# Moving the decay work of two of five token pieces out of the projection stage and into the first eight recurrence steps

## The chip, the cores and the metric

The kernel is one launch on one core of a Trainium2 chip. The metric is the device time of that launch in microseconds (us). The kernel before took 1749.78 us as the median of three runs (1746.99 to 1754.63).

The engines are named as in the profile: PE (TensorE, matmul), PEld (its weight loads), DVE (VectorE), ACT (ScalarE), POOL (GpSimd) and SP (SyncE, which here issues nearly all DMAs from one queue, in order).

## The reference, cut to what matters

One layer of a diffusion backbone over 1024 latent tokens and 256 context tokens of width 1024. One input projection is split between a short convolution group and a bidirectional RWKV-7 group of 8 heads of 64; both are concatenated, projected and added to the input, and a gated MLP with a 3x3 depthwise convolution follows. What matters here is the RWKV part:

```
cb, cc, cx, r, k, v, w_lo, a_lo, g_lo = split(h @ w_in)
kk = k * k_k, normalized over each head
for d in 0, 1:                       # forward and backward in time
    decay = exp(-c * sigmoid(w0[d] + tanh(w_lo) @ w_up[d]))
    a     = sigmoid(a0[d] + a_lo @ a_up[d])
    k_d   = k * (1 + (a - 1) * k_a)
    # per token, state S of each head (64 x 64):
    S = S * decay - (S kk) (kk a)^T + v k_d^T ;   y = S r
```

The context is scanned first, in both directions; the latent scans start from its final states. The backward scan runs from the last latent token to the first.

## The kernel before, in words

Every matmul of weights is done in three products of high and low parts of both operands. The program is written with a library that gives each tile its buffers and orders each engine's instructions by a planner of its own; each engine then runs its instructions strictly in that order and waits on semaphores. The order that is on the chip is therefore fixed when the program is built.

The stages, in order:

1. Modulation vectors and the normalized input (`norm_x`), until about 76 us of the profile.
2. Projections `proj` (L339 to L351), 24 matmuls for each block of 128 columns and 512 tokens. `k_cols` (L392) and `v_cols` (L440) come first, mixed with the rest of the modulation (`ada_rest`) and the normalization of k (`unit_k`), in the order of the string `OR1` (L46). v is transposed to token-major on PE and stored.
3. Decays. The 1280 tokens fall into five pieces of 256, named by their first tile of 128 tokens: piece 0 is the context, pieces 2, 4, 6 and 8 are the latents. `decays` (L520) does, for one piece, eight groups: four pairs of heads `j`, two directions `d` each. A group is four matmuls into `plo` (L551, L552), two tanh on ACT (L555), a sum and a scan on DVE (L558, L560 or L562), two exponentials on ACT (L566, L567), scaled copies of kk, r, k and b on POOL and DVE (L571 to L579), sixteen small matmuls into two `px` tiles (L597), their masking on DVE into `xa` and `xrO` (L599, L601), four transposes into `pt` (L605) and a copy (L607). The results go to memory (`ar_dram`, `xr_dram`, `kb_dram`).
4. Inversion. `invert` (L648) inverts the 64 x 64 triangular systems of one piece that `decays` left in `xa`. On DVE: a transpose, 30 pairs of multiply and add (L666, L668), each of which needs the one before, and two transposes. Then two rounds of small matmuls on PE, `pq` (L684) and `pr` (L691), with copies by ACT between them, and a store to `xa_dram` (L696).
5. The other projections: r and the gate (`r_and_gate`, L796) and the convolution group (`conv_group`, L809), 17 blocks of columns. In the program they stand between and after the pieces 0, 2, 8, 4, 6; the planner fills them in beside the decays.
6. Recurrence. `steps` (L712) does one step: one chunk of 64 tokens forward and one backward. It loads the chunk's data (`cxa` from `xa_dram`, `ckb`, `car`, `cxr`, `vu`), then `ry` (L733, L741), a copy `rh` (L743), `pu` (L750), a copy `vu` (L755, L757), `ps` (L764) and the state update `S` (L767), each waiting for the one before; `ry` (L773) gives y. Steps 1 to 4 are the context (piece 0), steps 5 to 8 need pieces 2 (forward) and 8 (backward), and from step 9 on one direction needs piece 4 and the other piece 6. There are 20 steps. `fill` (L701) puts parts of other work, held in the list `pend`, behind a step's matmuls, in the numbers given by `sl`: first the output product of the convolution group (`conv_out`, L882, tiles `pco`), later the rest of the output (`mix`, `outp`, `to_h2`).
7. The MLP (`pf`, L1038 and L1118), and the final norm.

PSUM has eight banks, and a `Banks` object (L112) says which banks serve which tile name. In the decay stage `B1` (L42) gives `px` banks 4, 5 and 1, `pl` (the tiles `plo` and `pbn`) banks 6 and 7, and `pq` bank 0. Two names on one bank take it in the order in which the program asks for it.

The lines on which the order of the stages rests:

```
decay_and_invert(0)                      # L839
...
for ti in (2, 8, 4, 6):
    decay_and_invert(ti)
...
for r in range(4):                       # L985: the context steps
    steps(ring, [(0, r // 2, r % 2), (1, 1 - r // 2, 1 - r % 2)], ppc, 1)
...
for r in range(16):                      # L992: the latent steps
```

Of the kernel before, what the change touches and what calls it, by code (L numbers as in the profile page):

```python
# [28 lines left out]
TAIL = {10: "m3 m4", 11: "o3 o4 h3 h4", 12: "m2 m5", 13: "o2 o5 h2 h5", 14: "m1 m6", 15: "o1 h1 o6 h6", 16: "m0 m7", 17: "o0 o7", 18: "h0 h7"}  # L29
SL = ((3, 2, 0, 1),) * 10 + ((4, 4, 4, 4),) * 6  # L30
RC = 9
EI = 3
FAST, FQ = (0, 7), (1,)
B5 = dict(pm=(5, 7), px=(0, 4), ph=(4, 0))
YT = 3
IB = 2
XB, XT = 2, 3
# [3 lines left out]
AE = (0, 1, 0, 1, 0, 0, 1, 0)  # L41
B1 = ((4, 5, 1), (2, 3), (6, 7), (0,), (1,))  # L42
B2 = ((2, 3), (1, 6))
B3 = (7, 5)
PA, PL1 = (0,), (6,)
OR1 = "k0 k1 a k2 a k3 a u 0 a u a 1 u a a x 2 a 3"  # L46
B4 = dict(pm=(5, 7), px=(0,), ph=(4,))
# [39 lines left out]
def hybrid_kernel(  # L87
# [238 lines left out]

    cols = [3072] + [b + 128 * j for b in (2048, 2560, 1536) for j in range(4)] + [3200]
    cols += [b + 128 * j for j in range(4) for b in (512, 1024, 0)]
# [30 lines left out]
    def stg():  # L359
        return sg_.tile([128, 512], F32, name="stg", bufs=STG)  # L360
# [38 lines left out]
    def unit_k():  # L399
# [7 lines left out]
        for t0, nt in ((0, 2), (2, 4), (6, 4)):  # L407
# [30 lines left out]
            yield  # L438

    def v_cols(j):  # L440
        for t0, n, p in proj(pp, 2560 + 128 * j, True, 6):
            vt = stg()
            A.copy(vt[:, :n], p[:, :n])
            vm = stg().rearrange("p (t n) -> p t n", n=128)
            nt = n // 128
            pv = pp.tile([128, 512], F32, name="pv", tag="pv", bufs=2)
            for q in range(nt):
                PE.transpose(pv[:, 128 * q:128 * q + 128], vt[:, 128 * q:128 * q + 128], ident)
            V.tensor_copy(vm[:, :nt, :], pv[:, :n].rearrange("p (t n) -> p t n", n=128))
            SY.dma_start(vd[t0 // 128:t0 // 128 + nt, :, 128 * j:128 * j + 128].rearrange("t p n -> p t n"), vm[:, :nt, :])  # L450
# [69 lines left out]
    def decays(pp, pieces):  # L520


        for ti in pieces:
# [4 lines left out]
            for j in range(4):  # L528
# [265 lines left out]

    ppc = Banks(px=B1[0], pj=B1[1], pl=B1[2], pq=B1[3], ry=B1[4], pu=B1[4])
    def r_and_gate():  # L796
        for j in range(4):
            for t0, n, p in proj(ppc, 1536 + 128 * j, False, 6):
                rt = stg()
                A.copy(rt, p)  # L800
                SY.dma_start(rd[j, :, t0 - CTX:t0 - CTX + n], rt)
            yield
# [4 lines left out]
        yield  # L807

# [46 lines left out]
    sh2 = ExitStack()  # L855
    h2p = sh2.enter_context(tc.tile_pool(name="h2p", bufs=1, side="left", reuse_waits="tile"))
    h2 = [[h2p.tile([128, 8, 512], F32R, name=f"h2{hf}{i}") for i in range(2)] for hf in range(2)]
    so = ExitStack()
    ow = so.enter_context(tc.tile_pool(name="ow", bufs=1, side="left", reuse_waits="tile"))

# [324 lines left out]
```

## Time and profile before

| | |
|---|---|
| median of 3 runs | 1749.78 us |
| the profiled execution | 1747.66 us |
| its span, first to last instruction | 1745.9 us |
| PE busy | 1588.5 us (91% of the span) |
| DVE busy | 1146.1 us (66%) |
| ACT busy | 565.3 us (32%) |
| POOL busy | 610.4 us (35%) |
| mean granted PE clock | 0.933 |
| share of the chain that ended last | PE 67%, DVE 18%, DMA 6%, issue 3%, ACT 3%, POOL 2% |

Times are of one execution, read by the hardware profiler. A matmul's busy time overlaps with the next one's, so the pace of PE is read from the starts of its rows. "Granted clock" is 1.0 where PE ran at 2.4 GHz and 0.5 where it ran at 1.2 GHz; a stretch's value is the mean.

### The profile page before, as it was taken

The numbers are of one execution on the slowest core, as the hardware profiler recorded it, in microseconds if no ns is written. First come the engines' busy times: TensorE is split into PE (matmuls) and PEld (weight loads), VectorE is DVE, ScalarE is ACT, GpSimd is POOL, SyncE is SP. The second block draws the span as 40 slices with busy tenths as digits, with TensorE's granted clock in tenths as the row PEclk, the third lists the DMA queues.
The fourth block names the chain that finished last, engine by engine and source line by source line (L and its number), as shares of the span: only waits on it lengthen the run. The fifth ranks groups of instructions, "written<-read, shape, count | busy, mean of one in ns | idle before, by whom it ended". The sixth has DMA issues, their size and how long they took to land.

```text
span 1745.9 us, 27316 instructions
## 1 busy us (share of the span) xinstructions
PE 1588.5 (91%) x10639; PEld 1272.3 (73%) x10639; DVE 1146.1 (66%) x1791; ACT 565.3 (32%) x994; POOL 610.4 (35%) x519
## 2 busy tenths in 40 slices
PE   7699999989898967698687999999999999999997
PEld 2588778777777766577565777888888888788886
DVE  5953525799999983333677667766666666545645
ACT  2644315544535323211133332111111111334423
POOL 2343313333333224723443422222222222545643
PEclk9799799989889966889889999999999999999999
DMA  9294536557667387789863421111111111533531
GB/s 316 99 298 153 178 124 186 180 156 218 203 187 233 103 254 234 244 259 291 266 209 120 128 70 37 49 48 49 49 47 40 47 48 49 169 109 118 172 97 61
DMA packets 237178, 257.41 MB, mean 147 GB/s; under 512 B 18932, under 2 KB 172105, under 8 KB 237049
## 3 DMA queue, kind: packets, MB, share of 16 engines
q1 hardware_dynamic: 236664, 255.51, 46.9%
q8 instruction: 84, 1.38, 0.3%
q14 instruction: 46, 0.37, 0.1%
q0 software_dynamic: 384, 0.15, 0.0%
HBM read 184.04 MB, written 71.57 MB: 146 GB/s over the span
## 4 chain that ended last, share of the span: by engine, by line
PE 67%; DVE 18%; DMA 6%; issue 3%; ACT 3%; POOL 2%; SPq 1%; DVEq 0%; POOLq 0%; ACTq 0%
PE pf L1038 26%; PE pf L1118 14%; PE pj L350 12%; DVE ti L668 3%; DVE tmp L666 3%; PE pco L878 2%; PE po L878 2%; DMA araw<-in_ada_w_dram 2%; PE px L597 1%; DVE acc L1085 1%; PE ry L741 1%; DMA xo<-in_w_out_dram 1%; PE pu L750 1%; PE ps L764 1%; DVE xrO L601 1%
## 5 line engine op out<-in xcount | busy, mean ns | idle before, releaser
L1038 PE MATMUL pf<-h,fhi 128*128 128x512 f32 x1408 | 395.7, 397 | 6.0 <-DVE act L1090 3.4
L1038 PEld LDWEIGHTS pf<-h,fhi 128*128 128x128 f32 x1408 | 264.6, 188 | 70.3 <-DVE act L1090 3.8
L350 PE MATMUL pj<-hx,whi 128*128 128x512 f32 (+1 forms) x976 | 303.4, 390 | 1.5 <-DVE hx L324 1.5
L1085 DVE SCALAR_TENSOR_TENSOR acc<-gp,prm,acc 128x1024 f32<-128x1024 f32 x176 | 270.5, 1538 | 6.0
L105 POOL TENSOR_TENSOR flo<-fraw,fhi 128x1024 fp32r<-128x1024 f32 x50 | 139.1, 2782 | 331.5 <-ACT fhi L104 323.1
L1038 PE MATMUL pf<-h,flo 128*128 128x512 f32 x704 | 227.5, 395 | 0.5 <-POOL flo L105 0.5
L350 PEld LDWEIGHTS pj<-hx,whi 128*128 128x128 f32 x976 | 185.4, 198 | 38.3 <-issue 4.2
L350 PE MATMUL pj<-hx,wlo 128*128 128x512 f32 (+1 forms) x488 | 189.7, 389 | 0.0
L1118 PE MATMUL pf<-dhi,ahl 128*128 128x512 f32 x640 | 163.2, 389 | 0.0
L1038 PEld LDWEIGHTS pf<-h,flo 128*128 128x128 f32 x704 | 132.5, 188 | 34.0 <-POOL flo L105 0.8
L1110 DVE TENSOR_TENSOR ahl<-act,ahl 128x512 fp32r<-128x512 f32 x44 | 86.3, 1971 | 97.2 <-ACT ahl L1109 97.2
L104 ACT CAST fhi<-fraw 128x1024 fp32r<-128x1024 f32 x50 | 52.5, 1049 | 285.8 <-issue 164.4
L1118 PEld LDWEIGHTS pf<-dhi,ahl 128*128 128x128 f32 x640 | 120.1, 188 | 25.4 <-DVE ahl L1110 0.4
L105 POOL TENSOR_TENSOR dlo<-fraw,dhi 128x1024 fp32r<-128x1024 f32 x40 | 98.1, 2458 | 88.5 <-ACT dhi L104 88.4
L105 POOL TENSOR_TENSOR wlo<-wraw,whi 128x1024 fp32r<-128x1024 f32 x26 | 63.9, 2458 | 168.5 <-ACT whi L104 168.4
L1083 DVE TENSOR_SCALAR acc<-gp,prm 128x1024 f32<-128x1024 f32 x22 | 42.6, 1936 | 111.6 <-ACT gp L1075 111.6
L350 PEld LDWEIGHTS pj<-hx,wlo 128*128 128x128 f32 x488 | 96.4, 198 | 17.5 <-issue 1.7
L1118 PE MATMUL pf<-dlo,ahl 128*128 128x512 f32 x320 | 89.1, 389 | 0.0
L597 PE MATMUL px<-arO,kbO 64*128 64x128 f32 (+1 forms) x640 | 66.5, 318 | 18.9 <-DVE xrO L601 12.1
L597 PEld LDWEIGHTS px<-arO,kbO 64*128 64x128 f32 x640 | 54.0, 214 | 35.5 <-issue 29.2
L104 ACT CAST dhi<-fraw 128x1024 fp32r<-128x1024 f32 x40 | 41.9, 1047 | 107.0 <-PE pf L1118 87.5
L760 POOL TENSOR_TENSOR S<-S,pcs 128x512 f32<-128x512 f32 x38 | 41.2, 1099 | 95.8 <-PE ry L741 94.9
(280 smaller groups left out, 2649.2 us busy)
## 6 DMA issues: line engine op xcount, KB each, us to landing
araw<-in_ada_w_dram SPq DMA_DIRECT2D x48, 512.0 KB, 5.2
fraw<-in_ffn_w_up_dram SPq DMA_DIRECT2D x46, 512.0 KB, 3.9
fraw<-in_ffn_w_down_dram SPq DMA_DIRECT2D x44, 512.0 KB, 3.6
wraw<-in_w_in_dram SPq DMA_DIRECT2D x26, 512.0 KB, 4.5
lu<-lu_dram SPq DMA_DIRECT2D x20, 512.0 KB, 5.2
kb_dram<-kbT SPq DMA_DIRECT2D x40, 256.0 KB, 2.7
xa_dram<-xa SPq DMA_DIRECT2D x20, 512.0 KB, 4.8
cxa<-xa_dram SPq DMA_DIRECT2D x40, 256.0 KB, 4.2
```

The source lines that it names most:

```text
L104: A.copy(hi, src)
L105: G.tensor_tensor(out=lo, in0=src, in1=hi.bitcast(F32), op=ALU.subtract)
L350: PE.matmul(p[:, :n], w[:, k, :], hsl(i, k, t0, n), start=(k == 0 and first), stop=(k == 7 and last))
L597: PE.matmul(px[:, ch, i, 0:w], kbO[r, i, 2 * ch:2 * ch + 2, :].rearrange("p s n -> p (s n)"), rhs, start=True, stop=True)
L666: V.tensor_tensor(out=tv, in0=ti[:, j + 1:32, j:j + 1].to_broadcast([128, m, j]), in1=ti[:, j:j + 1, 0:j].to_broadcast([128, m, j]), op=AL ...
L668: V.tensor_tensor(out=ti[:, j + 1:32, 0:j], in0=ti[:, j + 1:32, 0:j], in1=tv, op=ALU.add)
L878: m = PE.matmul(po, hl[:, a_, k, :], w[k][b_][:, sl], start=(k == 0 and f), stop=(k == 3 and l))
L1038: PE.matmul(pts[hf], w[:, k, :], h2[hf][i_][:, k, :], start=(k == 0 and f), stop=(k == 7 and l))
L1083: V.tensor_scalar(out=acc, in0=src, scalar1=wcol, scalar2=prm[:, P_FB + f:P_FB + f + 1], op0=ALU.mult, op1=ALU.add)
L1085: V.scalar_tensor_tensor(out=acc, in0=src, scalar=wcol, in1=acc, op0=ALU.mult, op1=ALU.add)
L1110: V.tensor_tensor(out=hl[:, 1, :], in0=asl, in1=hl[:, 0, :].bitcast(F32), op=ALU.subtract)
L1118: PE.matmul(pd[i], hl[:, a_, 128 * q:128 * q + 128], w[w_][:, 512 * nh:512 * nh + 512], start=(f == 0 and s_), stop=(f == NF - 1 and l_))
```

## The change

The pieces are prepared in another order and at another place.

- The r projections move to stage 2, where the v projections were (`OR1`, `r_cols`, `cols`); the v projections move behind the decays of the end pieces.
- Of the decays and inversions, pieces 0, 2 and 8 alone stand in the program ahead of the recurrence, and behind them v, the gate and the convolution group.
- Pieces 4 and 6 become a generator, `rest`. After each of the first eight steps five parts of it are issued (`PCS`); a piece has 8 parts of decays and 11 of inversion. Steps 9 to 20 come when `rest` is empty, and the second half of the output weights (`wr`) is loaded between.
- In the first eight steps a fill of 1, 1, 0, 1 (`SL0`) parts of `conv_out` stands behind each step's matmuls, from the first step on.
- Banks: in the decay stage `pl` has bank 6 alone and `pv` bank 7; in the first eight steps `px` has banks 4 and 5, and bank 7 serves `pl` and `pq` both.
- Buffers: the inversion's tiles go from two buffers to one (`IB`), `dr` to one, and `rk` shares the buffer of `db`.

```
-IB = 2
+SL0, PCS = (1, 1, 0, 1), 5
+IB = 1
-B1 = ((4, 5, 1), (2, 3), (6, 7), (0,), (1,))
+B1 = ((4, 5, 1), (2, 3), (6,), (0,), (7,))
-OR1 = "k0 k1 a k2 a k3 a u 0 a u a 1 u a a x 2 a 3"
+OR1 = "k0 k1 a k2 a k3 a u r0 a u a a r1 u a a x r2 r3"
-    cols = [3072] + [b + 128 * j for b in (2048, 2560, 1536) for j in range(4)] + [3200]
+    cols = [3072] + [b + 128 * j for b in (2048, 1536, 2560) for j in range(4)] + [3200]
+    def r_cols(j):
+        for t0, n, p in proj(pp, 1536 + 128 * j, False, 6):
+            rt = stg()
+            A.copy(rt, p)
+            SY.dma_start(rd[j, :, t0 - CTX:t0 - CTX + n], rt)
...
-                    rt = dq.tile([128, NP], F32, name="dr")
+                    rt = dq.tile([128, NP], F32, name="dr", bufs=1)
-                    rk = dq.tile([128, NP], F32, name="rk", bufs=1)
+                    rk = dq.tile([128, NP], F32, name="rk", tag="db", bufs=1)
...
-    ppc = Banks(px=B1[0], pj=B1[1], pl=B1[2], pq=B1[3], ry=B1[4], pu=B1[4])
+    ppc = pp = Banks(px=B1[0], pj=B1[1], pl=B1[2], pq=B1[3], pv=B1[4])
...
-    decay_and_invert(0)
-    for _ in range(4):
-        next(rg)
-    for ti in (2, 8, 4, 6):
-        decay_and_invert(ti)
-    for _ in rg:
-        pass
-    for _ in cg:
-        pass
+    def decay_and_invert(pp, ti):
+        yield from decays(pp, (ti,))
+        yield from invert(pp, ti)
+    for ti in (0, 2, 8):
+        for _ in decay_and_invert(ppc, ti):
+            pass
+    for j in range(4):
+        v_cols(j)
+    gate_cols()
+    for _ in conv_group():
+        pass
...
-    ppc = Banks(ry=B2[0], pu=B2[1])
-    for r in range(4):
-        steps(ring, [(0, r // 2, r % 2), (1, 1 - r // 2, 1 - r % 2)], ppc, 1)
-        if r == 0:
-            pend.append(conv_out())
-            next(pend[0])
-            wr = [w_load(ow, 4 + k, (G, V)[k % 2]) for k in range(4)]
+    pp = Banks(pa=(0,), ry=(2, 3), pu=(1, 6), px=(4, 5), pl=(7,), pq=(7,))
+    rest = (p for ti in (4, 6) for p in decay_and_invert(pp, ti))
+    pend.append(conv_out())
+    next(pend[0])
+    chunks = [[(0, r // 2, r % 2), (1, 1 - r // 2, 1 - r % 2)] for r in range(4)]
+    chunks += [[(0, 2 + r // 2, r % 2), (1, 9 - r // 2, 1 - r % 2)] for r in range(4)]
+    for z in chunks:
+        steps(ring, z, pp, 2, SL0)
+        for _ in range(PCS):
+            next(rest, None)
+    for _ in rest:
+        pass
...
+    wr = [w_load(ow, 4 + k, (G, V)[k % 2]) for k in range(4)]
-    for r in range(16):
+    for r in range(4, 16):
```

What the planner makes of it is seen in each engine's order. Line numbers in the order of the change are its own; the tile names say which instruction it is.

PE, just ahead of the first matmul of the recurrence (`ry`). Before, it comes when the last projection (`pj`) and the last `px` of the last piece are done:

```order
L350 MATMUL pj<-hx,wlo 128x512
L597 MATMUL px<-arO,kbO 128x128 x7
L350 MATMUL pj<-hx,whi 128x512
L684 MATMUL pq<-rti,xa 32x32 x32
L605 MATMUL pt<-cst,kbO 128x128 x4
L350 MATMUL pj<-hx,wlo 128x512
L597 MATMUL px<-arO,kbO 128x128 x8
L684 MATMUL pq<-rti,xa 32x32 x32
L691 MATMUL pr<-xr,qs 32x32 x32
L733 MATMUL ry<-vu,cxa 64x64
```

In the change:

```order
L691 MATMUL pq<-rti,xa 32x32 x32
L604 MATMUL px<-arO,kbO 128x128 x8
L612 MATMUL pt<-cst,kbO 128x128 x4
L698 MATMUL pr<-xr,qs 32x32 x32
L604 MATMUL px<-arO,kbO 128x128 x8
L612 MATMUL pt<-cst,kbO 128x128 x4
L740 MATMUL ry<-vu,cxa 64x64 x3
L698 MATMUL pr<-xr,qs 32x32 x32
L740 MATMUL ry<-vu,cxa 64x64 x13
```

All projections stand ahead of the first `ry` in both. Before, all 40 groups and the inversions of four pieces stand there too; in the change 20 groups and the inversions of two pieces do (piece 0, piece 2 and the first four groups of piece 8).

DVE, from the eighth `rh` copy to the ninth. Before, these are all the rows there are:

```order
L743 COPY rh<-ry 64x512
L896 TENSOR_TENSOR xo<-pco,xo 128x512 x2
L757 TENSOR_SCALAR vu<-pu 64x512
L896 TENSOR_TENSOR xo<-pco,xo 128x512 x2
L767 TENSOR_TENSOR S_2048<-ps,S_2048 64x4x64 x2
L767 TENSOR_TENSOR S_2050<-ps,S_2050 64x4x64 x2
L889 TENSOR_TENSOR chl<-chl 128x512
L743 COPY rh<-ry 64x512
```

In the change 184 rows stand there: the state update of step 8, the second half of piece 4's inversion, all eight groups of piece 6 and the whole of piece 6's inversion. This is where the inversion of piece 4 ends and the first group of piece 6 begins:

```order
L673 TENSOR_TENSOR tmp<-ti 128x30
L675 TENSOR_TENSOR ti<-ti,tmp 128x30
L679 STREAM_TRANSPOSE xr<-ti 128x32x32
L681 STREAM_TRANSPOSE rti<-ti 128x32x32
L684 COPY xa<-xr 32x32x32 x2
L550 COPY bon<-pbn 128x2x2
L565 TENSOR_SCALAR sw<-sw 128x256
L567 SCALAR_TENSOR_TENSOR sw<-rst,sw 128x256
L582 SCALAR_TENSOR_TENSOR db<-da,dkk 128x256
L583 TENSOR_TENSOR kbO<-db,sw 128x2x128
```

No row of a step stands between these and the ninth `rh`.

PE at the same place in the change, from the last `ry` of step 8 on (`pco` is one part of `conv_out`):

```order
L780 MATMUL ry<-vu,cxr 64x64 x15
L870 MATMUL pco<-wh_5169,chl 128x512
L870 MATMUL pco<-wl_5170,chl 128x512
L870 MATMUL pco<-wh_5169,chl 128x512
L691 MATMUL pq<-rti,xa 32x32 x64
L698 MATMUL pr<-xr,qs 32x32 x64
L549 MATMUL pbn<-hsr,rk 128x2 x2
L740 MATMUL ry<-vu,cxa 64x64
L558 MATMUL plo<-dxl,lu 128x256
L559 MATMUL plo<-dxl,lu 128x256
```

The first `plo` of piece 6 stands behind piece 4's `pq` and `pr`, and behind one `ry` of step 9, which reads piece 4's inverse from memory.

## Rows read from the trace of the kernel before

**Rows 1.** By stage: us, busy PE, PEld, DVE, ACT, POOL, clock, DMA share, GB/s.

```profile
76.00:261.50 185.50, 184.29 (x876) 144.20 (x875) 87.72 (x133) 72.79 (x123) 52.32 (x35) 0.92 0.56 183
261.50:620.40 358.90, 329.68 (x2773) 268.90 (x2772) 311.10 (x709) 172.58 (x325) 120.10 (x181) 0.92 0.61 185
620.40:629.10 8.70, 6.66 (x113) 6.08 (x113) 7.90 (x25) 1.95 (x4) 0.74 (x1) 0.55 1.00 318
629.10:742.00 112.90, 76.86 (x1202) 67.17 (x1202) 56.71 (x96) 28.61 (x42) 60.22 (x43) 0.75 0.77 239
```

**Rows 2.** Chain that ended last, one decay group: start, us, what.

```profile
283.65 3.40 PE pj L350 x15
287.05 0.36 PE px L597 x2
...
287.85 1.03 PE px L597 x14
288.88 0.59 PE pt L605 x4
289.47 0.12 PE plo L551
...
289.93 3.44 PE pj L350 x15
```

**Rows 3.** PE in order of time: inversion matmuls and `px`: start, us.

```profile
608.97 1.20 PE L684 MATMUL pq<-rti,xa 32*32 32x32 f32 x64 [0.96 <-DVE rti L674]
...
611.54 2.70 PE L597 MATMUL px<-arO,kbO 64*128 64x128 f32 x16 [0.55 <-DVE xrO L601]
614.17 1.92 PE L684 MATMUL pq<-rti,xa 32*32 32x32 f32 x64
```

**Rows 4.** DVE busy on tile `sw`, over the whole span.

```profile
0.00:1745.90 1745.90, 77.78 (x160) 50.20 (x120) 0.93 0.47 147
```

**Rows 5.** PE, PEld and DVE busy on tile `px`, over the whole span.

```profile
0.00:1745.90 1745.90, 66.51 (x640) 54.03 (x640) 52.31 (x144) 0.93 0.47 147
```

**Rows 6.** Groups of DVE by line: busy us, mean ns, idle before.

```profile
L575 DVE SCALAR_TENSOR_TENSOR db<-da,dkk 128x256 f32<-128x256 f32 x40 | 19.5, 486 | 8.9 <-ACT da L555 8.4
L578 DVE TENSOR_TENSOR da<-da,dk 128x256 f32<-128x256 f32 x40 | 16.7, 416 | 0.9 <-ACT da L577 0.8
L743 DVE COPY rh<-ry 64x512 f32<-64x512 f32 x20 | 13.8, 688 | 45.2 <-PE ry L741 30.1 <-issue 8.2 <-ACT rh L743 4.0
L767 DVE TENSOR_TENSOR S<-ps,S 64x256 f32<-64x256 f32 x80 | 33.7, 421 | 16.9 <-PE ps L764 15.3
```

**Rows 7.** DVE busy on tile `ti`, over the whole span, all five inversions.

```profile
0.00:1745.90 1745.90, 160.71 (x320) 0.93 0.47 147
```

**Rows 8.** DVE busy on tile `ti`, in the last inversion alone.

```profile
615.30:671.50 56.20, 28.99 (x64) 0.67 0.75 229
```

**Rows 9.** The last inversion in order of time, DVE and ACT.

```profile
615.34 1.39 DVE L656 COPY xb<-xa 32x1024 f32<-32x1024 f32 x2
...
635.41 0.40 DVE L666 TENSOR_TENSOR tmp<-ti 128x234 f32<-128x234 f32 x1
...
655.54 1.95 DVE L674 STREAM_TRANSPOSE rti<-ti 128x1024 f32<-128x1024 f32 x1
...
670.28 1.17 ACT L693 COPY xa<-pr 32x512 f32<-32x512 f32 x2 [1.01 <-PE pr L691]
```

**Rows 10.** DVE's copy `rh` of the first and of the ninth step.

```profile
629.09 0.68 DVE L743 COPY rh<-ry 64x512 f32<-64x512 f32 x1
...
741.73 0.70 DVE L743 COPY rh<-ry 64x512 f32<-64x512 f32 x1
```

**Rows 11.** DMA issues: count, KB each, us from issue to landing.

```profile
xa_dram<-xa SPq DMA_DIRECT2D x20, 512.0 KB, 4.8
...
cxa<-xa_dram SPq DMA_DIRECT2D x40, 256.0 KB, 4.2
```

More of the change, by code (lines that the diff above doesn't have):

```diff
@@ L502, in hybrid_kernel @@
         else:
-            v_cols(int(o))
+            r_cols(int(o[1:]))
     for _ in ada_:
@@ L506, in hybrid_kernel @@
     sa.close()
-    shc.close()
-    wp = sh.enter_context(tc.tile_pool(name="wp", bufs=1, side="right", reuse_waits="tile"))
+    sw_ = ExitStack()
+    wp = sw_.enter_context(tc.tile_pool(name="wp", bufs=1, side="right", reuse_waits="tile"))
     st = ss_.enter_context(tc.tile_pool(name="st", bufs=1, side="left", reuse_waits="tile"))
@@ L793, in steps, with gate_cols @@
                 SY.dma_start(yd[t], e_[0])
-    ppc = Banks(px=B1[0], pj=B1[1], pl=B1[2], pq=B1[3], ry=B1[4], pu=B1[4])
[L796 to L802, printed above, removed]
+    ppc = pp = Banks(px=B1[0], pj=B1[1], pl=B1[2], pq=B1[3], pv=B1[4])
+    def gate_cols():
         for t0, n, p in proj(ppc, 3200, False, 4):
@@ L806, in r_and_gate @@
             SY.dma_start(sgd[:, t0 - CTX:t0 - CTX + n], sgt)
-        yield
     def conv_group():
@@ L829, in conv_group @@
             yield
-    rg, cg = r_and_gate(), conv_group()
-    def decay_and_invert(ti):
-        for _ in decays(ppc, (ti,)):
-            pass
-        for _ in invert(ppc, ti):
-            pass
-    decay_and_invert(0)
-    for _ in range(4):
-        next(rg)
-    for ti in (2, 8, 4, 6):
-        decay_and_invert(ti)
-    for _ in rg:
-        pass
-    for _ in cg:
-        pass
+    def decay_and_invert(pp, ti):
[3 more added lines that the diff above has]
+        for _ in decay_and_invert(ppc, ti):
+            pass
+    for j in range(4):
+        v_cols(j)
+    gate_cols()
+    for _ in conv_group():
+        pass
+    sw_.close()
+    shc.close()
     sh.close()
-    sx.close()
-    pp = Banks(pa=B3, ry=(2, 3), pu=(1, 6), **B4)
     srB = ExitStack()
@@ L854, in hybrid_kernel @@
     cp_ = sa.enter_context(tc.tile_pool(name="co", bufs=1, side="right", reuse_waits="tile"))
[L855 to L859, printed above, removed]
     gb1 = cp_.tile([128, D], F32, name="gb1")
@@ L983, in hybrid_kernel @@
     stages = {"m": mix, "o": outp, "h": to_h2}
-    ppc = Banks(ry=B2[0], pu=B2[1])
-    for r in range(4):
-        steps(ring, [(0, r // 2, r % 2), (1, 1 - r // 2, 1 - r % 2)], ppc, 1)
-        if r == 0:
-            pend.append(conv_out())
-            next(pend[0])
-            wr = [w_load(ow, 4 + k, (G, V)[k % 2]) for k in range(4)]
+    pp = Banks(pa=(0,), ry=(2, 3), pu=(1, 6), px=(4, 5), pl=(7,), pq=(7,))
[10 more added lines that the diff above has]
+        pass
+    sx.close()
+    pp = Banks(pa=B3, ry=(2, 3), pu=(1, 6), **B4)
+    sh2 = ExitStack()
+    h2p = sh2.enter_context(tc.tile_pool(name="h2p", bufs=1, side="left", reuse_waits="tile"))
+    h2 = [[h2p.tile([128, 8, 512], F32R, name=f"h2{hf}{i}") for i in range(2)] for hf in range(2)]
+    so = ExitStack()
+    ow = so.enter_context(tc.tile_pool(name="ow", bufs=1, side="left", reuse_waits="tile"))
+    wr = [w_load(ow, 4 + k, (G, V)[k % 2]) for k in range(4)]
     plan = dict(TAIL)
-    for r in range(16):
+    for r in range(4, 16):
         for o in plan.get(r, "").split():
```

## The prediction

> **What bounds the kernel now.** I read the busy time by stage first, then the chain of waits inside the decay stage, then DVE's rows, because the order of the change moves DVE's work most. In the table by stage [rows 1] the second row is the stretch from the first low-rank matmul of the decays to the first `ry` of the recurrence (261.5 to 620.4, 358.9 us): PE is busy 329.7 us at a mean clock of 0.92, and DVE 311.1 us, a share of 0.87. Both are nearly full. The fourth row is the stretch of the first eight steps: DVE is busy 56.7 of 112.9 us, PE 76.9 at a clock of 0.75. So there is room on DVE in the steps, about 56 us, and the question is whether what the change puts there is less than that room plus what it takes from ahead of `ry`. In the chain [rows 2] a decay group goes by at PE's pace: 15 projection matmuls 3.40 us, `px` 0.36 and 1.03, `pt` 0.59, `plo` four times 0.12, and the next group's projections at 289.93, so 6.28 us a group, filled by projections.
>
> I make the sum for the profiled execution, 1747.7 us (1.8 beyond its span, 2.1 below the median of three). Two stretches change: up to the first `ry`, and from the first `rh` copy to the ninth.
>
> **Up to the first `ry`.** PE's work there at full speed: 787 projection matmuls at 3.40/15 = 0.227 us are 178.5; 40 groups at 1.39 + 0.59 + 0.48 = 2.46 us [rows 2] are 98; 7.5 rounds of `pq` or `pr` at 1.20 [rows 3] are 9. Sum 286, so 73 of the 358.9 us are lost: 29 idle and 44 to a clock below full [rows 1]. In the change 20 groups (49 us) and two inversions with two rounds of `pq` and two of `pr` each (10 us) are gone from here, which leaves 227. How much of the 73 is lost then? DVE's work per group is 77.78/40 = 1.94 on `sw` [rows 4], 4 masks at 52.31/144 = 0.363 [rows 5], 0.486 and 0.416 for `db` and `da` [rows 6], 4.30 together; per inversion 160.71/5 = 32.1 on `ti` [rows 7] and two pairs of copies at 1.39 [rows 9], 34.9. So DVE loses 86 + 70 = 156 of its 311 us and has 155 to do in some 245. PE will seldom wait for it. In the stage ahead of this one, where PE has projections and DVE is busy 87.7 of 185.5 us, PE is busy 184.3 [rows 1]. I take a loss of 15 us, nearer to that row; the ends are 0 and half of the 73, 36, since half the groups stay. Moving r before v costs in stage 2 about ten longer matmul drains; I take 2 us. First `ry` earlier by 359 − (227 + 15) − 2 = 115 us, ends 94 and 130. All projections still stand ahead of `ry` on PE, so 130 is a ceiling. `ry` should start near 506.
>
> **From the first `rh` to the ninth.** Before: 629.09 to 741.73, 112.6 us [rows 10]. The order on DVE puts in this stretch 20 groups at 4.30 (86 us), 3 inversions at 34.9 (105), the 8 steps' own work at 0.69 for `rh`, as much for `vu` of the same shape and 4 × 0.421 for `S` [rows 6], 3.06 (25), and some nine other operations (8): 224 us. About 135 of them stand before the eighth `rh` and 89 behind it.
>
> First to eighth `rh`: DVE sets the pace. Its share when loaded is 0.91 in the third row and 0.87 in the second [rows 1]; 135/0.91 = 148 us, ends 135 (no gap) and 165 (0.82, since each step's chain of `ry`, `rh`, `pu`, `vu`, `ps`, `S` goes through DVE's in-order queue behind pieces of inversion, and pieces of inversion behind it).
>
> Eighth to ninth `rh`: no row of a step stands between the end of piece 4's inversion and the ninth `rh` on DVE, and on PE the first `plo` of piece 6 stands behind piece 4's `pq` and `pr`, since bank 7 serves `pl` and `pq` both. So the parts follow each other:
>
> - the rest of piece 4's inversion on DVE, from about 635.41 to 657.49 in the last inversion of before [rows 9], less a step's 3: 19;
> - its `pq` and `pr` rounds with ACT's copies, 657.49 to 671.45: 14;
> - its way through memory, 4.8 for the store and 4.2 for the load [rows 11], because one `ry` that reads piece 4's inverse stands ahead of piece 6's first `plo`: 9;
> - eight groups of piece 6: 50 at the pace of 6.28 [rows 2]; ends 34, DVE's own 4.30 each, and 61, if `px` takes 2.70 us after a wait [rows 3] where it takes 1.39 in the chain;
> - piece 6's inversion, 615.34 to 671.45 [rows 9], less two steps' work in it, 7: 49;
> - memory again 9, and the `ry` of step 9, 3.
>
> That is 153 us; ends 137 (34 for the groups) and 164 (61). The stretch takes 148 + 153 = 301 instead of 112.6: +188. This is the step on which the forecast hangs: 89 us of DVE work cost 153 because nothing stands beside them.
>
> On the clock, the row of `px` that began after a wait of 0.55 us took 2.70 [rows 3], and the steps run at 0.75 where the decay stage has 0.92 [rows 1]: PE falls to the lower of its two levels when it has gaps. In the Trainium skill, "TensorE: Matmul & The Clock Gate" (Part 1) has the same rule, a clock that is held down by default and released by sustained matmul work, and it speaks against leaving piece 6 with no projections beside it. By the row's price for all eight groups the sum is 8 × 1.31 = 10 us higher, 1833; I leave it as an end, as the groups' own pace may be DVE's.
>
> **The rest.** The second half of the output weights is loaded in steps 9 to 11 now, with POOL's share ahead of its part in the state updates: 0, ends −8 (DMA freed in the steps before) and +15 (a few operations of POOL in front of `S`). `conv_out` moves to the same steps in smaller parts and is hidden by DVE's work there. With one buffer for the inversion's tiles the inversions can't overlap each other: on DVE they don't anyway. Steps 10 to 20 and the MLP stay.
>
> **Sum.** 1747.7 − 115 + 188 = 1821 us. Ends: −130 + 135 + 137 − 113 = +29, and with −8 about 1769; −94 + 165 + 164 − 113 = +122, and with +15 about 1885.
>
> **Rivals.**
>
> (a) VectorE's busy sum alone sets the stretch. Then the 224 us run without a gap and faster, as POOL is quieter: on `ti` the last inversion took 28.99 [rows 8] against a mean of 32.1 [rows 7], so two of the three inversions are 3 us shorter: 218. With no loss ahead of `ry`: −130 + 218 − 113 = −25, 1723 us, faster. For it: 0.91 in the loaded stretch. Against: the order itself, in which DVE has to wait for PE and ACT once per group of piece 6 and for four rounds of PE and ACT after the inversions. It decides only if DVE is busy over 0.97 of the time from the first `rh` to the ninth; at 0.87 with the same prefix the change is already slower. The Trainium skill, "SBUF — State Buffer" (on who interferes with whom), has VectorE and GpSimd share a port for which one blocks the other; the two rows on `ti` agree with it, and by them the forecast would be 6 us lower, 1815. Chance 0.08.
>
> (b) The wait at bank 7 and the drain of the inversions are hidden, so that eighth to ninth `rh` takes DVE's 89 and two trips of 9 through memory, 107. Then −115 + 148 + 107 − 113 = +27, 1775 us. For it: DVE takes only 4.30 of 6.28 us a group. Against: the `plo` behind `pq` on PE's queue. Chance 0.08.
>
> (c) SP's queue holds the steps. SP issues nearly all DMAs in order; each chunk's loads stand behind the decays' stores, and a store waits for its producer. If in seven steps the loads come a landing time late, 4.2 to 4.8 us [rows 11], that is +32: 1853 us. For it: in the steps SP now has the stores of 20 groups besides. Against: the steps wait for DVE anyway, and the loads are asked for two steps ahead. Chance 0.11.
>
> (d) The change does not do what its words say: the fill is five parts a step, 40 in all, of 38 for two pieces with the inversion of piece 8 besides; the order shows that piece 6 is not beside the steps but behind them. That is in the forecast.
>
> **How the numbers follow.** The forecast has 0.73, (a) 0.08, (b) 0.08, (c) 0.11. Likeliest 1821. What a measurement of this kernel can tell from no change is 0.5%, 8.7 us. Faster by more needs a loss ahead of `ry` near nothing and a full DVE together: (a), 0.07. Within 0.5%, between (a) and the low end of the forecast: 0.05. Slower: 0.88. Eight times in ten the time should lie between 1768 (the low ends together, and (b)) and 1870 ((c), and most of the high ends).
>
> **What would show it.** Right: first `ry` between 491 and 526; 135 to 165 us from first to eighth `rh`, with DVE busy above 0.85; 137 to 164 from the eighth to the ninth, with DVE busy near 0.6, DVE waiting for PE's `px` or `plo` once a group, and PE at a lower clock than 0.75 there; the first `plo` of piece 6 released by ACT's copy of `pr` or by the load of piece 4's inverse. Wrong: DVE without gaps between the eighth and ninth `rh` (then (a) or (b)); steps 1 to 8 that wait for `cxa`, `car` or `ckb` with DVE idle (then (c)); a first `ry` later than 535; or steps 9 to 20 longer by more than 15 us.

## The result, and the profile after

The changed kernel takes 1856.69 us (median of four runs, 1854.88 to 1857.92) against 1748.38: a ratio of 1.0615, 95% interval 1.0582 to 1.0648. That is 108 us slower, where the forecast had 73, inside its range. The profiled execution has a span of 1854.7 us.

The same stretches as in [rows 1], now cut at the first `plo` of the decays, the first `ry`, and the first, eighth, ninth and twentieth `rh` (window, us, busy PE, PEld, DVE, ACT, POOL, clock, DMA share, GB/s):

```profile
260.80:520.20 259.40, 240.90 (x1764) 199.78 (x1762) 184.53 (x368) 102.92 (x179) 78.78 (x97) 0.95 0.51 150
520.20:527.50 7.30, 7.30 (x119) 6.63 (x118) 1.35 (x5) 2.84 (x5) 1.25 (x2) 0.65 1.02 309
527.50:709.70 182.20, 134.95 (x1519) 110.31 (x1519) 141.31 (x280) 59.50 (x111) 66.83 (x87) 0.72 0.69 212
709.70:861.20 151.50, 70.40 (x873) 58.72 (x874) 83.13 (x192) 40.85 (x76) 22.25 (x38) 0.53 0.36 114
861.20:1052.70 191.50, 154.86 (x1913) 125.53 (x1911) 109.79 (x214) 49.25 (x106) 74.25 (x67) 0.89 0.77 243
```

| term | forecast | measured |
|---|---|---|
| first `rh` earlier (629.1 before, 527.5 after) | 115 | 101.6 |
| first to eighth `rh` (112.6 before) | 148 | 182.2 |
| eighth to ninth `rh` (19.3 before) | 153 | 151.5 |
| both together against before | +188 (against 112.6) | +201.7 (against 132.0) |
| from the ninth `rh` to the end (984.8 before, 993.5 after) | 0 | +8.7 |
| sum | +73 | +108.8 |

The 112.6 of the forecast is a misread row. [rows 10] takes the copy at 741.73 for the ninth `rh`, but counted from 629.09 it is the eighth: the rows behind it are those that the order of before lists behind the eighth. The ninth comes at 761.06. DVE's rows of before, and the stretch up to the right row:

```profile
742.46 1.29 DVE L896 TENSOR_TENSOR xo<-pco,xo 128x512 f32<-128x512 f32 x2
744.48 0.69 DVE L757 TENSOR_SCALAR vu<-pu 64x512 f32<-64x512 f32 x1 [0.74 <-PE pu L750]
...
755.27 0.69 DVE L889 TENSOR_TENSOR chl<-chl 128x512 fp32r<-128x512 f32 x1 [1.14 <-ACT chl L888]
761.06 0.68 DVE L743 COPY rh<-ry 64x512 f32<-64x512 f32 x1 [5.09 <-PE ry L741]
```

```profile
629.10:761.10 132.00, 93.86 (x1376) 81.69 (x1377) 62.93 (x107) 31.56 (x47) 61.87 (x44) 0.76 0.77 240
```

DVE's work from the first to the ninth `rh` is 141.3 + 83.1 = 224.4 us, the 224 of the forecast. What was off is the time around it, and the time of before that it was set against.

Ahead of `ry`. The last projection starts at 496.9, and PE's rows behind it show a tail that has none (start, us, what, and in brackets the idle time before it and who ended it):

```profile
497.13 0.28 PE L558 MATMUL plo<-dxl,lu 128*128 128x256 f32 x1
...
503.69 1.92 PE L691 MATMUL pq<-rti,xa 32*32 32x32 f32 x64 [5.05 <-DVE rti L681]
...
512.26 2.08 PE L604 MATMUL px<-arO,kbO 64*128 64x128 f32 x16 [3.47 <-DVE kbO L586]
...
520.22 0.69 PE L740 MATMUL ry<-vu,cxa 64*64 64x64 f32 x6
```

From 497 to 520 PE is at 0.60 of its clock, and waits for the inversion of piece 2 and for two groups of piece 8:

```profile
497.00:520.00 23.00, 13.33 (x240) 11.45 (x238) 18.43 (x30) 11.85 (x20) 12.59 (x11) 0.60 0.92 260
```

In the first step. DVE's rows from the first `rh` on:

```profile
527.50 0.68 DVE L750 COPY rh<-ry 64x512 f32<-64x512 f32 x1 [0.86 <-PE ry L748]
532.61 2.04 DVE L565 TENSOR_SCALAR sw<-sw 128x256 f32<-128x256 f32 x1 [4.43 <-ACT sw L562]
534.69 2.71 DVE L567 TENSOR_TENSOR_SCAN sw<-rst,sw 128x256 f32<-128x256 f32 x1
...
540.29 2.52 DVE L583 TENSOR_TENSOR kbO<-db,sw 128x256 f32<-128x256 f32 x1
...
545.22 0.69 DVE L583 TENSOR_TENSOR kbO<-db,sw 128x256 f32<-128x256 f32 x1 [0.62 <-ACT sw L574]
...
573.72 0.67 DVE L764 TENSOR_SCALAR vu<-pu 64x512 f32<-64x512 f32 x1
...
581.64 0.69 DVE L750 COPY rh<-ry 64x512 f32<-64x512 f32 x1
```

46 us lie between `rh` and `vu` of the first step, in which DVE works off four groups of piece 8, the ones left over, and the start of its inversion. The step stands in the queue behind them. From the first to the second `rh` it takes 54 us, from the seventh to the eighth 15.

Behind the eighth step. PE's rows at bank 7, where piece 4's inversion ends and piece 6 begins:

```profile
727.28 1.92 PE L691 MATMUL pq<-rti,xa 32*32 32x32 f32 x64 [9.22 <-DVE rti L681]
730.47 1.91 PE L691 MATMUL pq<-rti,xa 32*32 32x32 f32 x64 [1.27 <-ACT qs L693]
733.65 1.91 PE L698 MATMUL pr<-xr,qs 32*32 32x32 f32 x64 [1.27 <-ACT qs L693]
736.85 1.92 PE L698 MATMUL pr<-xr,qs 32*32 32x32 f32 x64 [1.28 <-ACT xa L700]
740.04 1.01 PE L549 MATMUL pbn<-hsr,rk 128*128 128x2 f32 x4 [1.27 <-ACT xa L700]
742.67 0.47 PE L740 MATMUL ry<-vu,cxa 64*64 64x64 f32 x2 [1.61 <-DMA cxa<-xa_dram]
743.07 0.58 PE L558 MATMUL plo<-dxl,lu 128*128 128x256 f32 x1
```

And the chain that ended last, in the groups that follow (start, us, what):

```profile
752.54 2.83 DMA dr<-r_dram
755.53 0.73 POOL rk L546
756.31 1.02 PE pbn L549 x4
757.32 2.00 PE px L604 x14
759.33 0.51 PE plo L558
...
768.97 3.94 DMA dr<-r_dram
```

Two groups take 16.4 us. Once in two groups the chain goes through the load of `dr` and the product `rk`; in the change `dr` has one buffer, and `rk` shares one with `db`.

### The profile page after: what moved, and what is told of

Same layout as the page of the kernel before. It is cut to its first block, busy times and chain, and to the rows that moved or that the text cites. A ratio compares the mean times of both kernels' runs of the same rounds, so it can differ in the third digit from the quotient of the medians.

```text
span 1854.7 us, 27195 instructions
## 1 busy us (share of the span) xinstructions
PE 1615.9 (87%) x10639; PEld 1293.8 (70%) x10639; DVE 1171.9 (63%) x1791; ACT 570.5 (31%) x994; POOL 605.1 (33%) x519
## 4 chain that ended last, share of the span: by engine, by line
PE 50%; DVE 15%; DMA 6%; issue 3%; ACT 3%; POOL 2%; SPq 1%; DVEq 0%; POOLq 0%; ACTq 0%
PE pf L1044 25%; PE pf L1124 11%; PE pj L351 3%; DVE tmp L673 2%; DVE ti L675 2%; PE pco L870 2%; DVE acc L1091 1%; PE px L604 1%; PE po L870 1%; PE ry L748 1%; DMA chl<-yc_dram 1%; DVE S L774 1%; PE ry L740 1%; PE pu L757 1%; DMA dr<-r_dram 1%
## 5 line engine op out<-in xcount | busy, mean ns | idle before, releaser
L351 PE MATMUL pj<-hx,whi 128*128 128x512 f32 (+1 forms) x976 | 298.6, 387 | 1.5 <-DVE hx L325 1.5
L604 PE MATMUL px<-arO,kbO 64*128 64x128 f32 (+1 forms) x640 | 70.0, 357 | 19.3 <-DVE kbO L586 16.9
L604 PEld LDWEIGHTS px<-arO,kbO 64*128 64x128 f32 x640 | 58.8, 251 | 30.5 <-issue 16.1
L575 POOL COPY pcs<-P 128x4 f32<-128x4 f32 x40 | 9.0, 226 | 215.4 <-ACT P L573 215.4
```

Source lines behind the costliest of these rows:

```text
L351: PE.matmul(p[:, :n], w[:, k, :], hsl(i, k, t0, n), start=(k == 0 and first), stop=(k == 7 and last))
L604: PE.matmul(px[:, ch, i, 0:w], kbO[r, i, 2 * ch:2 * ch + 2, :].rearrange("p s n -> p (s n)"), rhs, start=True, stop=True)
```

## The experiments

Of each run, beside the median: how many of the 40 groups stand ahead of the last projection in PE's order (counted by their `pt`), the start of that projection, the first and the ninth `rh` (us of its trace), and what is left from the ninth `rh` to the end. Each ratio is to the median of the runs of before that were at hand, 1747 to 1748 us.

| run | median | groups | last `pj` | first `rh` | ninth `rh` | left |
|---|---|---|---|---|---|---|
| before | 1748 | 40 | 610.5 | 629.1 | 761.1 | 985 |
| after | 1857 | 18 | 496.9 | 527.5 | 861.2 | 994 |
| e1 decays first | 1829 | 18 | 498.7 | 531.0 | 831.1 | 996 |
| e2 piece 6 only | 1774 | 28 | 561.8 | 597.3 | 785.4 | 992 |
| e3 order of before | 1818 | 24 | 535.2 | 557.8 | 817.8 | 1000 |
| e4 buffers only | 1781 | 28 | 554.2 | 589.7 | 778.7 | 997 |
| e5 one dr | 1778 | 28 | 558.1 | 584.5 | 791.5 | 989 |
| e6 piece 6, own dr | 1762 | 32 | 570.8 | 602.3 | 766.4 | 995 |
| e7 both, own dr | 1789 | 24 | 542.4 | 565.9 | 785.2 | 1001 |
| e8 inversions only | 1767 | 35 | 587.7 | 634.1 | 758.0 | 1005 |
| e9 two banks | 1838 | 21 | 527.3 | 558.9 | 848.5 | 988 |
| e10 keep busy | 1858 | 18 | 492.6 | 523.4 | 859.9 | 992 |
| e11 one inversion buffer | 1756 | 36 | 601.5 | 631.8 | 773.1 | 985 |
| e12 fill earlier | 1743 | 40 | 605.9 | 623.9 | 755.5 | 981 |

The ninth `rh` carries most of the result: in the change it is 100 us later, of 109. An early first `rh` does not: e4 has it 39 us earlier than before and is 34 us slower. Behind the ninth `rh` the runs built on the change take 988 to 1005 us, and before, e5, e11 and e12 981 to 989. Where the loss is small this decides: e8 has its ninth `rh` 3 us earlier than before and is 19 us slower.

The count of groups goes with the time: 4 groups behind the last projection go with 9 us (e11), 8 with 14 (e6), 12 with 27 to 34 (e2, e4, e5), 16 with 41 or 70 (e7, e3), 22 with 82 or 108 (e1, after), so some 2 to 5 us each. It is a count beside the time and not a price: these runs differ in more than the groups.

**e1, decays first.**

```
-rest = (p for ti in (4, 6) for p in decay_and_invert(pp, ti))
+rest = (p for g in [decays(pp, (4,)), decays(pp, (6,)),
+                    invert(pp, 4), invert(pp, 6)] for p in g)
```

> The change with one edit: pieces 4 and 6 are issued as decays of 4, decays of 6, inversion of 4, inversion of 6, so that no decay group stands behind piece 4's pq and pr at bank 7. The stretch ahead of ry is the same, and so is DVE's work from the first to the ninth rh (some 224 us). Theory (piece 6 loses time because it runs alone behind bank 7): the drain of piece 4's inversion (23 us in the trace of the change, 727 to 742) and two or three of the eight groups at 8.2 us leave the stretch from the eighth to the ninth rh, and some 15 to 20 us come back in the steps before: 1825 to 1840 us against 1857. Rival (DVE's sum sets the pace, the bank costs nothing): 1852 to 1862.

1829.36 us, ratio to before 1.0465 (1.042 to 1.051). First to eighth `rh` 189.0 (182.2 in the change), eighth to ninth 111.2 (151.5). PE's rows of this run, behind the eighth `rh` (at 719.94):

```profile
725.92 0.69 PE L771 MATMUL ps<-vu,ckb 128*64 128x64 f32 x16
726.43 1.10 PE L780 MATMUL ry<-vu,cxr 128*64 128x64 f32 x30
...
728.35 1.16 PE L604 MATMUL px<-arO,kbO 64*128 64x128 f32 x16
729.45 0.61 PE L549 MATMUL pbn<-hsr,rk 128*128 128x2 f32 x4
```

Groups of piece 6 now run beside step 8, with nearly the same DVE work from the first to the ninth `rh` (217 us against 224). 40 us leave the serial stretch and 7 come back ahead of it. So the order in which the change issues groups and inversions cost 27 us net. Bank 7 is what that order passes through on PE, but a run with another bank and the same order was not made.

**e2, piece 6 only; e3, the order of before; e4, the buffers only.** Three kernels with v in stage 2, r behind, `B1` of before, and the change's buffers, fills and later weights. They differ in what is issued beside the steps (e2 and e4 with three parts a step, e3 with five):

```
 B1 = ((4, 5, 1), (2, 3), (6, 7), (0,), (1,))     # all three
 rest = decays and inversion of piece 6           # e2
 rest = the same of pieces 4 and 6                # e3
 rest = nothing; all five pieces ahead            # e4
```

> v stays in stage 2, r behind, pl keeps two banks and px three, as before; only piece 6 (decays and inversion) goes beside the first eight steps, piece 4 stays ahead of ry; the buffers and fills are those of the change. Theory (the time is lost where a piece's groups have no projections or step beside them, not by moving a piece): the first rh 45 to 55 us earlier than before, the first to the ninth rh 145 to 160 us instead of 113 (DVE has some 115 us of work there, and only the second half of one inversion with its drain, about 50 us, stands alone): 1735 to 1755 us. Rival (every piece that leaves the projections costs more in the steps than it saves ahead of them, in the ratio of the change, 210 against 102): half of the change's loss, 1795 to 1805 us.

> Both pieces move as in the change, but v stays in stage 2, r stands between the pieces and pl has two banks, as before, so that 25 groups instead of 20 stand ahead of ry in the order. Theory (34 of the 35 us that the forecast missed come from the last four groups and the inversion of piece 8, which the change's order leaves inside the first steps): first rh 10 to 20 us later than in the change, first to eighth rh 90 to 110 us instead of 182, eighth to ninth 150 to 165 as in the change: 1785 to 1805 us. Rival (the slow first steps are the price of pieces 4 and 6 themselves): first to eighth rh over 150 us, 1840 or more.

> All five pieces stand ahead of ry, in the order of before, with v in stage 2; only the change's buffers (one of each inversion tile, one dr, rk beside db), its fills and its later loading of the output weights stay. If the single buffers cost nothing: 1745 to 1755 us. If they do (a group of piece 6 in the change waits for dr and rk, 2.8 and 0.7 us once in two groups): 16 latent pairs of groups at 3.5 us, at most 56, partly hidden by projections: 1765 to 1800 us.

e2 1774.14 us (1.0139, 1.0091 to 1.0186), e3 1817.71 (1.039, 1.0351 to 1.0429), e4 1781.31 (1.0185, 1.0143 to 1.0227). e2 is over its expectation, since the buffers cost 34 us by themselves (e4). Beside e4, moving both pieces loses 36 us; moving piece 6 alone comes out 7 us lower, which is inside the spread of these runs (1765 to 1780 and 1777 to 1786). e3 is 13 us over its range, but its steps are as expected, first to eighth `rh` and eighth to ninth:

```profile
557.80:658.40 100.60, 88.37 (x1147) 71.77 (x1148) 70.51 (x148) 35.82 (x67) 48.26 (x59) 0.90 0.94 297
658.40:817.80 159.40, 71.27 (x878) 59.41 (x878) 91.12 (x204) 41.63 (x76) 26.26 (x41) 0.54 0.35 109
```

100.6 us where the change takes 182.2, though the same two pieces are issued beside these steps. So the slow first steps come from what the change's order of v and r and its banks leave over ahead of `ry`. The first `rh` is 30 us later for it, where 10 to 20 were expected, and 39 us remain as gain.

**e5, one `dr` only.** The kernel before, with

```
-rt = dq.tile([128, NP], F32, name="dr")
+rt = dq.tile([128, NP], F32, name="dr", bufs=1)
-rk = dq.tile([128, NP], F32, name="rk", bufs=1)
+rk = dq.tile([128, NP], F32, name="rk", tag="db", bufs=1)
```

> The kernel before with one edit: one buffer for dr and rk in db's buffer, as in the change. On DVE 32 groups stand ahead of the first rh in its order, as in the run with the change's buffers alone (1781), where before has 40. Theory (these two buffers make the 34 us of that run, because eight groups are left without projections beside them): 1770 to 1790 us. Rival (single inversion tiles, the fills or the later weights make them): 1745 to 1757 us.

1777.95 us (1.0169, 1.0151 to 1.0188): 30 of the 34 us of e4. Its stretch up to the last projection, the one behind it up to the second `rh`, and the one from there to the ninth:

```profile
261.00:558.10 297.10, 277.38 (x2040) 225.85 (x2039) 235.97 (x519) 130.69 (x242) 96.30 (x138) 0.95 0.57 172
558.10:685.80 127.70, 81.38 (x981) 68.39 (x979) 101.42 (x219) 52.82 (x96) 47.15 (x58) 0.59 0.70 215
685.80:791.50 105.70, 82.26 (x1259) 70.68 (x1258) 58.52 (x103) 25.56 (x39) 36.88 (x31) 0.79 0.72 227
```

In the order that is built with this edit the last projection starts 52 us earlier than before (558.1 against 610.5), and 12 of the 40 groups stand behind it, where before has none: 128 us at a clock of 0.59. Two 128x256 tiles decide this. PE's own waits for `rk` are 7.2 us ahead of that stretch and 8.2 in it, and how the 30 us divide between such waits and the new order was not separated. In that second stretch, who PE waited for (us in total, times, longest):

```profile
PE px L597 <- POOL car L646: 9.4, 1, 9.4
PE plo L551 <- DVE bon L543: 8.6, 2, 6.1
PE pbn L542 <- POOL rk L539: 8.2, 4, 4.9
```

**e6, piece 6 with its own `dr`; e7, both pieces with it.** e2 and e3 with two buffers for `dr`, one of its own for `rk`, and one staging buffer of the projections less:

```
-STG, WR, RB = 3, 1, 4
+STG, WR, RB = 2, 1, 4
-... name="dr", bufs=1)        -... name="rk", tag="db", bufs=1)
+... name="dr", bufs=2)        +... name="rk", bufs=1)
```

> Only piece 6 beside the first eight steps, as in e2, but two buffers for dr and rk in its own; one of the three staging buffers of the projections is given up for them. Ahead of the first rh 35 of 40 groups stand, and 107 us of DVE work from the first to the ninth. Theory (what e2 lost, 27 us, was these buffers): 1735 to 1752 us, no slower than before. Rival (moving a piece costs by itself): over 1760 us.

> Both pieces beside the steps with the order of before (e3), with two buffers for dr and rk in its own. In its order the whole inversion of piece 4 stands ahead of the eighth rh, so that its drain is no longer in series with piece 6. Theory: the eighth to the ninth rh 159 us in e3, here eight groups at 6.3 to 7 us, one inversion of 42 and 17 for memory and ry, 105 to 115; the rest about as e3: 1765 to 1785 us. Still slower than before, since piece 6 stands alone. Rival (the buffers matter only beside projections): 1800 or more.

e6 1762.06 us (1.0082, 1.0066 to 1.0098), 12 better than e2 but in the range of the rival: the first `rh` is 27 us earlier than before, the first to the ninth take 164 instead of 132. Some 14 us remain. In the trace 5 of 15 lie ahead of the ninth `rh` and 10 behind it. Up to 9 can be the single inversion buffers (e11 below), and the staging buffer given up was not tried alone, so what moving piece 6 costs by itself is small or nothing, and it is no gain. e7 1789.02 (1.0237, 1.0217 to 1.0257), 4 over its range. Its last stretch is as expected (106.4 us):

```profile
678.80:785.20 106.40, 50.70 (x618) 42.82 (x617) 69.73 (x160) 34.04 (x66) 23.73 (x39) 0.62 0.48 152
```

and the miss is ahead of it: the first `rh` 8 us later and first to eighth 112.8 instead of 100.6. The eight groups of piece 6 take 51.6 us from their first `plo` to their last `pt` (679.3 to 730.9), and in e3, with one `dr`, 63.7 (699.4 to 763.1).

**e8, inversions only.** e7 with all five pieces' decays ahead, three parts a step instead of five, and

```
-rest = (p for ti in (4, 6) for p in decay_and_invert(pp, ti))
+rest = (p for ti in (4, 6) for p in invert(pp, ti))
```

> All decays ahead of ry, in the order of before, with dr and rk as in before; only the inversions of pieces 4 and 6 are issued beside the first eight steps, three parts a step. DVE has some 82 us of work from the first to the ninth rh, in a stretch that took 113 us. Theory (DVE has room in the steps as long as nothing stands in series): the first rh 10 to 25 us earlier, the ninth not later than before, so 1725 to 1745 us, if the ninth rh is set by the inversion's chain, else 1745 to 1755. Rival (projections and not DVE set the stretch ahead of ry, so nothing is gained there, and the steps get slower): 1755 to 1770.

1767.26 us (1.0104, 1.0089 to 1.0119), the rival by its time, and half of it by its reason. Nothing is gained ahead of the steps: the last projection is 23 us earlier than before and the first `rh` 5 us later, since a tail stands between in which DVE has no gap at all:

```profile
587.70:612.80 25.10, 15.48 (x96) 12.35 (x94) 25.10 (x48) 9.61 (x20) 15.80 (x16) 0.68 0.99 297
```

But the steps with the inversions beside them are not slower: the first to the ninth `rh` takes 123.9 us instead of 132.0, so DVE has room there for the two inversions. The loss lies behind the ninth `rh`, 1005 us instead of 985, 15 of it up to the last `rh`. There PE waits 15.0 us for the copy `rh` (9.0 before) and 10.6 for `yt` (3.7). Why was not tested.

**e9, two banks for `pl`.** The change with

```
-B1 = ((4, 5, 1), (2, 3), (6,), (0,), (7,))
+B1 = ((4, 5), (2, 3), (6, 7), (0,), (1,))
```

> The change with one edit: in the stage of the projections pl has banks 6 and 7, pv bank 1, px banks 4 and 5 (the change gives pl bank 6 alone, px three). r still stands in stage 2 and v behind the end pieces. In its order 24 groups instead of 20 stand ahead of the first rh. Theory (the 39 us between the change and e3 come from pl's single bank, which spreads the groups so thin over the projections that four are left over): as e3, 1810 to 1825 us. Rival (they come from putting v where r was): 1845 to 1860.

1837.54 us (1.0526, 1.0505 to 1.0547), between the two: 19 of the 39 us come back. First to eighth `rh` 132.3 instead of 182.2, the first `rh` 31 later. The other 20 us up to e3 belong to v's place behind the pieces or to `px`' third bank, which e3 has and e9 has not; this was not separated.

**e10, PE kept busy.** The change, in the groups of piece 6 alone:

```
+if ti == 6:
+    for z in range(24):       # overwritten by the group's own matmuls
+        PE.matmul(pxs[z % 2][:, 0]..., lu[:, d, z % 4, :], xl[:, z % 2, :], ...)
```

> The change, with 24 more matmuls of 128x256 in each of piece 6's groups, into the px tiles that the group's own matmuls then overwrite. They need only data that is there, and keep PE busy while it would wait for DVE (some 2.9 us a group at full speed, 5.6 at the lower). If PE's lower clock (0.53 in this stretch) is what makes a group 8.2 us: the clock rises to 0.8 or more, a group takes 6.5 to 7.5, 1840 to 1852 us. If DVE, ACT, POOL and the load of dr make it: the clock may rise, but the stretch stays within 5 us or gets longer, 1852 to 1880.

1857.58 us (1.0641, 1.0616 to 1.0667), the same as the change. The eighth to the ninth `rh` (704.2 to 859.9) takes 155.7 us, with the groups from 740 to 812:

```profile
709.00:861.00 152.00, 77.18 (x998) 68.00 (x996) 79.56 (x179) 41.21 (x75) 24.89 (x39) 0.67 0.36 116
740.00:812.00 72.00, 49.35 (x366) 43.23 (x366) 40.86 (x92) 21.56 (x44) 18.96 (x34) 0.81 0.46 138
```

PE runs at 0.81 instead of 0.53 there, and nothing is gained. That does not price the clock. The 192 added matmuls take 29.8 us of PE, and in part they stand in series: the group's own `px` follows them without a gap, and DVE waits for it.

```profile
749.77 4.56 PE L601 MATMUL px<-dxl,lu 128*128 128x256 f32 x23
754.26 1.16 PE L607 MATMUL px<-arO,kbO 64*128 64x128 f32 x16
755.45 0.42 DVE L609 TENSOR_TENSOR xa<-px,cst 128x256 f32<-128x256 f32 x1 [5.34 <-PE px L607]
```

Such waits of DVE for `px` are 15.9 us in these groups, and 7.2 in the change. So the added matmuls may have taken back what the clock gave: a group's sixteen `px` took 1.16 us in the row above and 2.08 in the change (at 748.71).

**e11, one inversion buffer; e12, the fill earlier.** The kernel before with `IB = 1`; and the kernel before with

```
+    pend.append(conv_out())
+    next(pend[0])
     for r in range(4):
-        steps(ring, [...], ppc, 1)
-        if r == 0:   # conv_out and the weights wr
+        steps(ring, [...], ppc, 1, (1, 1, 0, 1))
     for r in range(16):
+        if r == 4:
+            wr = [w_load(ow, 4 + k, (G, V)[k % 2]) for k in range(4)]
```

> The kernel before with one edit: one buffer instead of two for the inversion's tiles. All 40 groups still stand ahead of the first rh, 18 of the 131 pairs of inversion operations move behind it. If single inversion buffers cost nothing: 1744 to 1753 us. If the later pairs leave room for the groups, up to 6 us less, and if the steps then wait for them, up to 15 more.

> The kernel before with the change's fills in the four context steps and its later loading of the output weights; the decays and inversions stay where they were. 24 matmuls of conv_out move from steps 13 and 14 to step 7, and POOL's and DVE's work on the weights leaves the first steps. In the runs so far the ninth to the last rh took 11 to 16 us less than before wherever conv_out was further ahead. Expected: 1738 to 1748 us, a little faster than before. Rival (the early steps lose what the later gain): 1746 to 1752.

e11 1756.46 us (1.006, 1.0039 to 1.008): the single inversion buffers cost 9 us, within the expectation's last case. e12 1743.34 (0.9981, 0.9966 to 0.9997): 4 us below before, in the expected range, at the edge of what these runs can tell, and the only version here below before. The reason that its expectation gives, 11 to 16 us less from the ninth to the last `rh` in earlier runs, rests on the misread row; against the right one, 187.6, none of them takes less (188.4 to 202.5). In e12's trace that stretch takes 183.8 us instead of 187.6, and the first `rh` comes 5 us earlier, though PE and DVE run the same order up to there: two executions of the same work differ by as much as the gain.

## Why the prediction was right, and where it was off

It was right in sign and in range, and 35 us short in size (73 of 108).

Part of that is luck. Of the 73 us, 19 are the time from the eighth to the ninth `rh` of before, which the forecast left out when it took 112.6 for 132.0. Its own terms with the right row give 1747.7 − 115 + 301 − 132 = 1802 us, 54 slower, half of what was measured; and its range of 1768 to 1870 would lie at 1749 to 1851, below the 1857. The three parts below were short by 13, 34 and −2 us, and the rest by 9.

**Up to the first `rh`: 115 forecast, 101.6 measured (100.2 to the first `ry`).** The term that was mis-sized is the loss of "15 us, nearer to that row": it was 32 (259.4 less the 227 of work), inside the end of 36. Most is the tail of 23 us behind the last projection, where PE is busy 13.3 us at a clock of 0.60. The forecast shared the projections evenly over the groups; the order spends them on 18 groups and leaves the other 22 without. DVE, too, had 184.5 us to do there and not 155: the 311 is busy time in which rows overlap, and the 156 taken from it is a sum of rows.

**First to eighth `rh`: 148 forecast, 182.2 measured, over the end of 165.** DVE's work was right (141 against 135), its share was not: 0.78 instead of 0.91, and under the 0.85 that was to show it. "DVE sets the pace" was taken from an 8.7 us stretch and from the decay stage with its projections [rows 1]. Here four groups of piece 8 stood alone, in DVE's queue ahead of the first step's `vu`, at 54 us for one step. e3 shows it: with 24 groups ahead of `rh` and `pl` on two banks the same stretch takes 100.6. This is the term that was mis-sized most, by 34 us.

**Eighth to ninth `rh`: 153 forecast, 151.5 measured.** The mechanism was right (e1 takes 40 us out of it by the order of groups and inversions alone), but parts of it cancel. The rest of piece 4's inversion and its rounds took 30 (709.7 to 740.0) against 33. Memory took 3 of the 9, to 743.1. The eight groups took 64 (743 to 807) against 50, over the end of 61, and piece 6's inversion 42 (807 to 849) against 49. The groups were slower by the buffers of `dr` and `rk`, which the forecast named nowhere as a cost: [rows 2] came from a kernel with two for `dr`, and with two the groups take 51.6 us (e7), where e3 with one has 63.7. Whether the lower clock, weighed as an end of 10 us, has a part in them stays open. In e10 the clock rose and the stretch was no shorter, but with 29.8 us of matmuls added. The Trainium skill, "TensorE: Matmul & The Clock Gate" (Part 1), says that work releases the clock, and e10's trace agrees (0.53 to 0.81). The inversion was faster beside a POOL that had 2 us of work in it. DVE's work on `ti`, which is all of this inversion:

```profile
740.00:861.00 121.00, 25.44 (x64) 0.52 0.41 128
```

25.4 us against 32.1 on average before [rows 7].

**The rest: 0 forecast, +8.7 measured**, inside its ends of −8 and +15. From the ninth to the last `rh` it is 191.5 us against 187.6, and 802.0 against 797.3 behind that. `conv_out` is hidden no better than before: 64 of its 192 matmuls stand ahead of the ninth `rh` in the change's trace, 76 before. The later weights and the fills of the first four steps alone are not the cause, since e12 has them and takes 981; the cause stays open.

**The rivals.** (a) needed DVE busy over 0.97; it is 224.4 of 333.7, 0.67. (b) needed the drain hidden; the rows at bank 7 show PE waiting through it, and e1, with part of it hidden, is still 82 us slower than before. (c) needed steps that wait for loads: from the first to the eighth `rh` PE waits once for `vu`, 4.1 us, and not for `cxa`, `car` or `ckb`. (d) stands as forecast.

**Where the 108 us are**, by medians: one buffer for `dr` and `rk` 30 (e5); the other buffers, fills and weights about 3 more (e4); both pieces moved 36 (e3 less e4); v behind r and the banks of stage 3 39 (the change less e3), of which 19 come back with `pl`'s second bank (e9). These are differences along one path of runs, and another path would share them otherwise: with two buffers for `dr`, moving both pieces is 41 us slower than before in all (e7). The move itself is about a third of the loss; the rest is what was given up to make room for it. Much of it shows as groups without projections beside them, which is read from the traces and was not varied by itself.

## What to carry to other kernels

Before moving work out of a stage, ask what it was covered by and what covers it in the new place: a chain that is cheap beside matmuls is paid at its full latency when it stands alone, which busy sums don't show. In the new order, count the groups that have lost their cover. Count what the move needs in buffers and banks and price those apart from the move, since in a program whose order is planned they change who stands beside whom. The time at which the dependent loop starts is worth little; find the point in it that needs the last piece, compare that, and then look at what follows. Count the rows of both traces when a step is picked by its number: one row off moved this forecast by 19 us.

## What the runs showed of the hardware

In the trace of the change POOL's long operations hold DVE up. POOL's rows on the output weights (start, us):

```profile
532.15 2.35 POOL L864 TENSOR_TENSOR wl<-xo,wh 128x1024 fp32r<-128x1024 f32 x1 [0.58 <-ACT wh L863]
534.46 2.40 POOL L862 TENSOR_TENSOR xo<-xo,gb 128x1024 f32<-128x1024 f32 x1
...
540.19 2.35 POOL L864 TENSOR_TENSOR wl<-xo,wh 128x1024 fp32r<-128x1024 f32 x1 [0.81 <-ACT wh L863]
```

Against DVE's rows shown above, `sw` began at 532.61 and took 2.04, the scan at 534.69 took 2.71, and `kbO` at 540.29 took 2.52, while the same `kbO` took 0.69 at 545.22. Each of the three long ones ends 0.1 to 0.6 us after the POOL operation beside it. The Trainium skill, "SBUF — State Buffer" (on who interferes with whom), says that the earlier of the two holds the port that they share for its whole instruction, and the later one blocks; these rows agree. In this trace one conversion of weights on POOL costs DVE up to 2 us.
